# Sums of weights for the MLPs' up products, made by adding DMAs instead of VectorE

## The chip, the cores and the metric

The kernel runs on one core of a Trainium2 chip. The core has a matrix engine (TensorE, PE in the profile; PEld is its loading of weights), three engines for elementwise work (VectorE or DVE, ScalarE or ACT, GpSimd or POOL), and SyncE (SP), which here only issues DMAs. Each engine works through its own queue in order; 16 DMA engines move data between DRAM and the core's memory (SBUF). Matmul results land in PSUM, in banks of 128 x 512 numbers. The metric is device microseconds of one execution.

## What is computed

The reference is a trunk of two residual layers over 1024 tokens of width 1024 (latent attention in the first, an mLSTM in the second), each followed by a gated MLP with a causal convolution of width 3. The change is in the MLP's first half:

```
def conv_ffn(h, w_up, conv_w, conv_b, w_down):
    a, g = jnp.split(h @ w_up, 2, axis=-1)
    a = lax.conv_general_dilated(a, conv_w[:, None, :], window_strides=(1,),
                                 padding=[(CONV_W - 1, 0)],
                                 dimension_numbers=('NWC', 'WIO', 'NWC'),
                                 feature_group_count=D_FF) + conv_b
    return (jax.nn.gelu(a, approximate=False) * g) @ w_down
```

`w_up` is 1024 x 5632: 2816 columns for a and 2816 for the gate g.

## The kernel before

Products are taken in float32r in three parts (`mm3`, lines 171 to 182): each operand is split into a high part, which ACT makes by a copy that rounds, and a low part, which DVE makes by subtracting the high part from the source; the three matmuls are high x high, high x low and low x high.

**Tiling of the up products.** The 2816 columns of a and of g are cut into 22 groups of 128 each (`FT`), and the 1024 tokens into two halves of 512. Per group the product is a 2 x 2 block product: the blocks of weights are a's lower and upper 512 rows and g's lower and upper 512 rows; the blocks of h are the lower and upper rows of the first half of the tokens (B11, B21) and of the second (B12, B22). It is done in the Winograd form of Strassen's scheme, with seven block products instead of eight. Four of the weight operands are sums of blocks, and four of the operands of h (T1 to T4) are sums too; these last are made once per MLP (`operands_second`, lines 932 to 963), T2, T3 and T4 by a generator `rest`, of which a piece is run after products 7, 8 and 10 (`REST`, line 1272).

**One step** is a pair of functions (`steps`, line 1084): one makes the weight operand, one runs the block product of twelve matmuls and takes the result out of PSUM.

| step | weight operand made by | product | result |
|---|---|---|---|
| 1 | `w_a`: loads a's weights | p1, with B11 | ACT copies bank A to a1 |
| 2 | a's upper rows | p2, with B21 | DVE adds to a1 |
| 5 | `w_s1`: loads g's weights; sum S1 | p5, with T1 | ACT copies bank D to g2 |
| 3 | `w_s4`: two subtractions | p3, with B22, on top of D | ACT copies D to a2 |
| 6 | S2 (made in `w_s4`) | p6, with T2, on top of A | DVE adds A to a2; convolution, gelu |
| 7 | `w_s3`: one subtraction | p7, with T3, on top of A | DVE adds A to g2; times t2; store |
| 4 | g's upper rows | p4, with T4, on top of A | DVE multiplies with t1; store |

The four sums are the DVE instructions of lines 1000, 1006, 1007 and 1011. `wop` (line 983) makes the high and low part of a weight operand (lines 988 and 989) in one half of a pair of tiles; four pairs rotate, so eight operands are alive, and a new pair waits until both products of the old pair are done.

**The order** is a list `seq` written out by hand (lines 1090 to 1098). The first four groups (`AHEAD`) run products 1 and 2 first, which need only the first half of the tokens, and then go in pairs; after that group n runs 5, 1, (7 of n - 1), 2, (4 of n - 1), 3, 6. The loop at line 1259 makes weight operands some products ahead (`LOOK`: 7 ahead in the first eight, then 5) and runs the product. A planner then puts each engine's instructions in order by its own estimate of when they are ready; `tc.high_priority()` moves the takings out of PSUM forward. Hooks run at given places of the list: loads and operands for the down products near its end (`ends`).

**Loads and buffers.** Weights come by SP into tiles `raw` of 128 x 1024 (`RAWS` = 5 buffers), sums go to tiles `wsum` (tag `wraw`, 2 buffers; each held S1 or S2 in one half and the other sums in the other). Groups 0 to 3 load a's weights twice (`again`, line 1004). Results go to DRAM (`u_d`) and come back as q for the down products. POOL has nothing but a memset of two columns per group (line 1042) and a small power per norm (line 255) here; in the down products it makes low parts of weights.

Of the kernel before, what the change touches and what calls it, by code (L numbers as in the profile page):

```python
# [18 lines left out]
P = 128  # L19
# [78 lines left out]
def trunk_kernel(ctx: ExitStack, tc: tile.TileContext, xT, pos, c_d, cols_d, mod_w, win, winT, w0, w1, wf, wd, out):  # L98
# [4 lines left out]
    def nm(s):  # L103
        n_names[0] += 1
        return f"{s}_{n_names[0]}"
# [807 lines left out]
    def two(t, k):  # L913
        return t[:, k:k + 2, :]

    def split_two(t, k, src):
        act.activation(two(t[0], k), src, AF.Copy)
        dve.tensor_tensor(two(t[1], k), src, two(t[0], k).bitcast(F32), ALU.subtract)

    def split_t(t, j, src, eng):  # L920
        act.activation(t[0][:, j, :], src, AF.Copy)
        eng.tensor_tensor(t[1][:, j, :], src, t[0][:, j, :].bitcast(F32), ALU.subtract)

    def operands_first(x, rb, l, hh, hl):

        for k in range(0, KT, 2):
            by_rows(x, k, rb)
            for i in (k, k + 1):
                h_of(x, i, l, x[:, i, :])
            split_two((hh, hl), k, two(x, k))  # L930

    def operands_second(px, xs, rb, l, T):

        x1, x2 = xs
        for k in range(0, KT, 2):
            by_rows(x2, k, rb)
            for i in (k, k + 1):
                h_of(x2, i, l, x2[:, i, :])
        low = (0, 2)
        for k in low:  # L940
            dve.tensor_tensor(two(x1, k), two(x2, k), two(x1, k), ALU.subtract)
            split_two(T["T1"], k, two(x1, k))
        for k in low:
            split_two(T["B22"], k, two(x2, k + 4))

        def rest():
            yield
            for k in low:
                dve.tensor_tensor(two(x1, k), two(x2, k + 4), two(x1, k), ALU.subtract)
                split_two(T["T2"], k, two(x1, k))  # L950
            yield
            for k in low:
                dve.tensor_tensor(two(x2, k), two(x2, k + 4), two(x2, k), ALU.subtract)
                split_two(T["T3"], k, two(x2, k))
            yield
            t4 = block(0, [P, KT, HS], F32R, "T4")
            T["T4"] = t4[:, 0:4], t4[:, 4:8]
            for k in low:
                dve.tensor_tensor(two(x1, k), two(x1, k + 4), two(x1, k), ALU.subtract)
                split_two(T["T4"], k, two(x1, k))  # L960

        T["rest"] = rest()
        next(T["rest"])

    def mlp(px, psC, T, l, u_d, pd, done, cols, extra=None, scaled=None):
# [9 lines left out]
        def raw(m, i):  # L975
            t = px.tile([P, 1024], F32, tag="raw", bufs=RAWS, name=nm("raw"))
            nc.sync.dma_start(t, wf[l, m, i])
            return t
# [4 lines left out]
        def wop(src, eng):  # L983
            if not room:
                t = [wp.tile([P, 1024], F32R, tag=f"w{j}", bufs=wbufs, name=nm(f"w{j}")) for j in ("hi", "lo")]
                room.extend([x[:, i * HS:(i + 1) * HS] for x in t] for i in range(2))
            hi, lo = [v[:, 0:src.shape[-1]] for v in room.pop(0)]
            act.activation(hi, src, AF.Copy)  # L988
            eng.tensor_tensor(lo, src, hi.bitcast(F32), ALU.subtract)  # L989
            return hi, lo  # L990

        def w_a(g):
            g["ra"] = raw(g["m"], 0)
            return wop(g["ra"][:, 0:HS], dve)

        def w_s1(g):
            g["rg"] = raw(g["m"], 1)
            t = wp.tile([P, 1024], F32, tag="wraw", bufs=wraws, name=nm("wsum"))
            g["s"], g["t"] = t[:, 0:HS], t[:, HS:]
            dve.tensor_tensor(g["s"], g["rg"][:, 0:HS], g["rg"][:, HS:], ALU.add)  # L1000
            return wop(g["s"], dve)

        def w_s4(g):
            if g["again"]:
                g["ra"] = raw(g["m"], 0)
            dve.tensor_tensor(g["s"], g["s"], g["ra"][:, 0:HS], ALU.subtract)
            dve.tensor_tensor(g["t"], g["ra"][:, HS:], g["s"], ALU.subtract)
            return wop(g["t"], dve)

        def w_s3(g):  # L1010
            dve.tensor_tensor(g["t"], g["ra"][:, 0:HS], g["rg"][:, 0:HS], ALU.subtract)
            return wop(g["t"], dve)

        def prod(ps, w, t, first):
            need(T["B11" if t in ("B11", "B21") else "T1"])
# [36 lines left out]
        def p5(g, w):  # L1052
            g["D"] = bank("pd")
            prod(g["D"], w, "T1", True)
            g["g2"] = pf.tile([P, HS], F32, tag="g2", bufs=2, name=nm("g2"))
            with tc.high_priority():
                act.activation(g["g2"], g["D"], AF.Copy)

        def p3(g, w):
            prod(g["D"], w, "B22", False)  # L1060
            a = g["a2"] = half_a(g)
            dve.tensor_copy(a[:, 0:2], g["a1"][:, HS:HS + 2])
            with tc.high_priority():
                act.activation(a[:, 2:], g["D"], AF.Copy)

        def p6(g, w):
            prod(g["A"], w, "T2", False)
            with tc.high_priority():
                dve.tensor_tensor(g["a2"][:, 2:], g["a2"][:, 2:], g["A"], ALU.add)
            g["t1"] = conv(g, g.pop("a1"))  # L1070
            g["t2"] = conv(g, g.pop("a2"))

        def p7(g, w):
            prod(g["A"], w, "T3", False)
            with tc.high_priority():
                dve.tensor_tensor(g["g2"], g["g2"], g["A"], ALU.add)
            out(g, 1, g["t2"], g["g2"])

        def p4(g, w):
            prod(g["A"], w, "T4", False)  # L1080
            with tc.high_priority():
                out(g, 0, g["t1"], g["A"])

        steps = {1: (w_a, p1), 2: (lambda g: wop(g["ra"][:, HS:], dve), p2), 3: (w_s4, p3),
                 4: (lambda g: wop(g["rg"][:, HS:], dve), p4), 5: (w_s1, p5),
                 6: (lambda g: wop(g["s"], dve), p6), 7: (w_s3, p7)}


        groups = [{"m": m, "again": m < AHEAD} for m in range(FT)]
        seq = [(k, g) for g in groups[:AHEAD] for k in (1, 2)]  # L1090
        a, b = groups[0:2], groups[2:4]
        for k, pair in ((5, a), (3, a), (6, a), (7, a), ((5, 4), b), (3, b), (6, b), (7, b), (4, b)):
            seq += [(k, g) for g in pair] if k != (5, 4) else [(5, b[0]), (5, b[1]), (4, a[0]), (4, a[1])]
        for n in range(AHEAD, FT):
            prev = (lambda k: [(k, groups[n - 1])]) if n > AHEAD else lambda k: []
            g = groups[n]
            seq += [(5, g), (1, g), *prev(7), (2, g), *prev(4), (3, g), (6, g)]
        seq += [(k, groups[-1]) for k in (7, 4)]
        seq = [(lambda k=k, g=g: steps[k][0](g), lambda w, k=k, g=g: steps[k][1](g, w)) for k, g in seq]
        ends = {k: len(seq) - 1 - i for i, k in enumerate((4, 7, 6, 3, 0, 2, 0, 1, 5))}  # L1100
        hooks = {}

        def hook(i, fn):
# [678 lines left out]
```

## Time and profile before

| what | us |
|---|---|
| time, median of 3 runs (lowest to highest) | 2197.75 (2197.21 to 2198.31) |
| span of the profiled execution | 2200.1 |
| PE busy in the span | 2166.5 |
| DVE busy in the span | 1693.1 |
| ACT busy in the span | 1046.7 |
| POOL busy in the span | 178.3 |

The profiled execution is one of its own; beside its span no time of it is given. The page shows for each engine the time in which an instruction of it ran. Matmuls overlap (each takes some 0.39 us, but one starts every 0.23 us), so PE's busy time is the time in which at least one ran. Rows of groups give the line of the kernel, the engine, what it writes from what, how often, the busy time and the mean of one, and the idle time just before with what ended it. Rows of the timeline give the start, the duration, the engine and line, and in brackets the idle time before it. The first MLP's up products run from about 486 to 906 us of the span, the second's from about 1547 to 1967.

### The profile page before, as it was taken

The numbers are of one execution on the slowest core, as the hardware profiler recorded it, in microseconds if no ns is written. First come the engines' busy times: TensorE is split into PE (matmuls) and PEld (weight loads), VectorE is DVE, ScalarE is ACT, GpSimd is POOL, SyncE is SP. The second block draws the span as 40 slices with busy tenths as digits, with TensorE's granted clock in tenths as the row PEclk, the third lists the DMA queues.
The fourth block names the chain that finished last, engine by engine and source line by source line (L and its number), as shares of the span: only waits on it lengthen the run. The fifth ranks groups of instructions, "written<-read, shape, count | busy, mean of one in ns | idle before, by whom it ended". The sixth has DMA issues, their size and how long they took to land.

```text
span 2200.1 us, 28740 instructions
## 1 busy us (share of the span) xinstructions
PE 2166.5 (98%) x10557; PEld 1818.0 (83%) x10557; DVE 1693.1 (77%) x2769; ACT 1046.7 (48%) x1812; POOL 178.3 (8%) x216
## 2 busy tenths in 40 slices
PE   9999999999999999999999999999999999999998
PEld 7878888787888888877888888988788888887787
DVE  8877878669878777899973655566887777778997
ACT  6465556446544444543453434344554444453335
POOL 0000000000000000042210111010000000002232
PEclk9999999999999999999999999999999999999999
DMA  8512234832444332542132243444143332245122
GB/s 317 152 50 63 92 109 142 285 125 69 157 139 143 123 125 85 204 151 89 53 121 93 62 131 103 132 157 171 64 144 101 111 120 92 79 163 194 50 80 77
DMA packets 105085, 270.50 MB, mean 123 GB/s; under 512 B 12336, under 2 KB 15984, under 8 KB 104944
## 3 DMA queue, kind: packets, MB, share of 16 engines
q1 hardware_dynamic: 104544, 268.28, 36.9%
q8 instruction: 83, 1.36, 0.3%
q14 instruction: 58, 0.48, 0.1%
q10 hardware_dynamic: 400, 0.39, 0.1%
HBM read 221.53 MB, written 44.47 MB: 121 GB/s over the span
## 4 chain that ended last, share of the span: by engine, by line
PE 85%; DVE 9%; DMA 3%; ACT 2%; issue 1%; POOL 0%; SPq 0%; POOLq 0%; DVEq 0%; ACTq 0%
PE pa L175 7%; PE pa L177 7%; PE pa L176 7%; PE pd L177 3%; PE pd L175 3%; PE pd L176 3%; PE sc L673 3%; PE op L175 3%; PE op L176 3%; PE op L177 2%; PE inp L177 2%; PE da L175 2%; PE inp L175 2%; PE inp L176 2%; PE da L176 2%; PE db L175 2%
## 5 line engine op out<-in xcount | busy, mean ns | idle before, releaser
L988 ACT ACTIVATE whi<-raw 128x512 fp32r<-128x512 f32 (+1 forms) x252 | 147.3, 607 | 243.2 <-PE pb L176 61.0
L988 ACT ACTIVATE whi<-wsum 128x512 fp32r<-128x512 f32 (+1 forms) x224 | 134.0, 617 | 181.8 <-PE pa L176 61.5
L175 PE MATMUL pa<-T,whi 128*128 128x512 f32 x528 | 205.9, 390 | 0.0
L176 PE MATMUL pa<-T,whi 128*128 128x512 f32 x528 | 205.4, 389 | 0.0
L177 PE MATMUL pa<-T,wlo 128*128 128x512 f32 x528 | 205.1, 389 | 0.0
L989 DVE TENSOR_TENSOR wlo<-wsum,whi 128x512 fp32r<-128x512 f32 (+1 forms) x224 | 151.1, 690 | 32.8 <-ACT whi L988 31.5
L989 POOL TENSOR_TENSOR wlo<-raw,whi 128x512 fp32r<-128x512 f32 (+1 forms) x80 | 119.9, 1515 | 401.7 <-ACT whi L988 394.0
L175 PE MATMUL da<-U,whi 128*128 128x512 f32 (+1 forms) x364 | 139.5, 383 | 3.4 <-DVE x L294 3.4
L177 PE MATMUL da<-U,wlo 128*128 128x512 f32 (+1 forms) x364 | 138.4, 383 | 2.0 <-DVE wlo L989 2.0
L176 PE MATMUL da<-U,whi 128*128 128x512 f32 (+1 forms) x364 | 139.2, 382 | 0.0
L989 DVE TENSOR_TENSOR wlo<-raw,whi 128x512 fp32r<-128x512 f32 (+1 forms) x172 | 115.7, 679 | 24.9 <-ACT whi L988 24.9
L167 ACT ACTIVATE whi<-wraw 128x1024 fp32r<-128x1024 f32 x67 | 70.7, 1059 | 117.1 <-PE op L176 59.2
L175 PEld LDWEIGHTS pa<-T,whi 128*128 128x128 f32 x528 | 99.1, 188 | 22.2 <-ACT whi L988 1.2
L177 PEld LDWEIGHTS pa<-T,wlo 128*128 128x128 f32 x528 | 99.1, 188 | 20.6
L176 PEld LDWEIGHTS pa<-T,whi 128*128 128x128 f32 x528 | 99.1, 188 | 20.3
L1140 DVE TENSOR_TENSOR U<-q,U 128x1024 fp32r<-128x1024 f32 x84 | 102.9, 1241 | 14.0 <-ACT U L1139 13.6
L1028 ACT ACTIVATE ct<-a,cols 128x512 f32<-128x512 f32 x88 | 70.8, 808 | 83.9 <-DVE a L1050 47.9
L175 PE MATMUL db<-U,whi 128*128 128x512 f32 x264 | 103.3, 391 | 1.3 <-ACT whi L988 1.3
L168 DVE TENSOR_TENSOR wlo<-wraw,whi 128x1024 fp32r<-128x1024 f32 x67 | 81.7, 1222 | 29.4 <-ACT whi L167 27.2
L177 PE MATMUL db<-U,wlo 128*128 128x512 f32 x264 | 102.9, 390 | 0.0
L176 PE MATMUL db<-U,whi 128*128 128x512 f32 x264 | 102.8, 389 | 0.0
L1139 ACT ACTIVATE U<-q 128x1024 fp32r<-128x1024 f32 x84 | 79.7, 979 | 47.7 <-DVE q L1138 22.2
(378 smaller groups left out, 6097.3 us busy)
## 6 DMA issues: line engine op xcount, KB each, us to landing
raw<-in_wf SPq DMA_DIRECT2D x96, 512.0 KB, 4.0
wraw<-in_w SPq DMA_DIRECT2D x67, 512.0 KB, 3.7
mraw<-in_mod_w SPq DMA_DIRECT2D x56, 512.0 KB, 4.0
ud<-ct SPq DMA_DIRECT2D x88, 256.0 KB, 2.4
q<-ud SPq DMA_DIRECT2D x88, 256.0 KB, 4.6
raw<-in_wd SPq DMA_DIRECT2D x32, 512.0 KB, 6.4
pa<-in_mod_w SPq DMA_DIRECT2D x24, 512.0 KB, 3.7
x<-xd SPq DMA_DIRECT2D x48, 256.0 KB, 4.8
```

Of the source, the lines that this page charges most:

```text
L167: act.activation(hi, raw, AF.Copy)
L168: dve.tensor_tensor(lo, raw, hi.bitcast(F32), ALU.subtract)
L175: pe.matmul(ps, lh, rh, start=first, stop=False, skip_group_check=more)
L176: pe.matmul(ps[:, 0:rl.shape[-1]], lh, rl, start=False, stop=False, skip_group_check=more)
L177: pe.matmul(ps, ll, rh, start=False, stop=last, skip_group_check=more)
L673: pe.matmul(ps[:, cs], a[:, qs if n < 3 else qrs_], b[:, cs], start=n == 0, stop=n == 4)
L988: act.activation(hi, src, AF.Copy)
L989: eng.tensor_tensor(lo, src, hi.bitcast(F32), ALU.subtract)
L1028: act.activation(t, a[:, 2:], AF.Identity, bias=col(f"cb{l}", m), scale=cw(m, 2))
L1139: act.activation(hi, w, AF.Copy)
L1140: dve.tensor_tensor(lo, w, hi.bitcast(F32), ALU.subtract)
```

## The change

The sums of weights are all made with plus signs, so that a DMA that adds to its destination can make them: `add_dma` issues from POOL a DMA with `accum_op=ALU.add`, which reads a block of weights in DRAM and adds it to what lies in SBUF. S1 is loaded as g's lower rows by SP, then g's upper rows are added. Step 5 splits it; then a's lower rows are added, which gives the operand of step 6; step 6 splits it; then a's upper rows are added, which gives the operand of step 3. The operand of step 7 is g's lower rows with a's lower rows added to them in place. To keep the result the same, the signs of T1, T2 and T4 are turned, g2 is taken with a factor of -1, the sum of product 7 is subtracted, and the last multiplication has a factor of -1 (`scalar_tensor_tensor` for `tensor_tensor`).

With it change: the order of steps 3 and 6 (6 first), and so T2 is made at once and B22 by the first piece of `rest`; a2 is copied from bank A after product 6, and D is added to it by DVE after product 3; two groups share a tile `wsum`, one half each; the loads of a group (a's and g's weights, the sum's first block and the two first adds) are issued ahead, at step 5 of the group before, or for the first groups at places given in `ahead` (`load`, `load_s`); the second load of a's weights for groups 0 to 3 is gone. Per group there are one more plain load of 256 KB on SP and four adding DMAs of 256 KB on POOL, and the four sums on DVE are gone.

```diff
...
         act.activation(t[0][:, j, :], src, AF.Copy)
         eng.tensor_tensor(t[1][:, j, :], src, t[0][:, j, :].bitcast(F32), ALU.subtract)
+    def neg_sub(out, a, b):
+        dve.scalar_tensor_tensor(out, a, -1.0, b, ALU.mult, ALU.subtract)
+    def add_dma(t, src):
+        pool.dma_start(t, src, accum_op=ALU.add)
     def operands_first(x, rb, l, hh, hl):
         for k in range(0, KT, 2):
...
                 h_of(x2, i, l, x2[:, i, :])
         low = (0, 2)
         for k in low:
-            dve.tensor_tensor(two(x1, k), two(x2, k), two(x1, k), ALU.subtract)
+            dve.tensor_tensor(two(x1, k), two(x1, k), two(x2, k), ALU.subtract)
             split_two(T["T1"], k, two(x1, k))
         for k in low:
-            split_two(T["B22"], k, two(x2, k + 4))
+            neg_sub(two(x1, k), two(x1, k), two(x2, k + 4))
+            split_two(T["T2"], k, two(x1, k))
         def rest():
             yield
             for k in low:
-                dve.tensor_tensor(two(x1, k), two(x2, k + 4), two(x1, k), ALU.subtract)
-                split_two(T["T2"], k, two(x1, k))
+                split_two(T["B22"], k, two(x2, k + 4))
             yield
             for k in low:
                 dve.tensor_tensor(two(x2, k), two(x2, k + 4), two(x2, k), ALU.subtract)
...
             t4 = block(0, [P, KT, HS], F32R, "T4")
             T["T4"] = t4[:, 0:4], t4[:, 4:8]
             for k in low:
-                dve.tensor_tensor(two(x1, k), two(x1, k + 4), two(x1, k), ALU.subtract)
+                neg_sub(two(x1, k), two(x1, k), two(x1, k + 4))
                 split_two(T["T4"], k, two(x1, k))
         T["rest"] = rest()
...
             eng.tensor_tensor(lo, src, hi.bitcast(F32), ALU.subtract)
             return hi, lo
+        halves_ = []
+        def load_a(g):
+            g["ra"] = raw(g["m"], 0)
+        def load_s(g):
+            m = g["m"]
+            if not halves_:
+                t = wp.tile([P, 1024], F32, tag="wraw", bufs=wraws, name=nm("wsum"))
+                halves_.extend(t[:, i * HS:(i + 1) * HS] for i in range(2))
+            g["rg"], g["s"] = raw(m, 1), halves_.pop(0)
+            nc.sync.dma_start(g["s"], wf[l, m, 1][:, 0:HS])
+            add_dma(g["s"], wf[l, m, 1][:, HS:])
+            add_dma(g["rg"][:, 0:HS], wf[l, m, 0][:, 0:HS])
+        def load(g):
+            load_a(g)
+            load_s(g)
         def w_a(g):
-            g["ra"] = raw(g["m"], 0)
+            if "ra" not in g:
+                load_a(g)
             return wop(g["ra"][:, 0:HS], dve)
         def w_s1(g):
-            g["rg"] = raw(g["m"], 1)
-            t = wp.tile([P, 1024], F32, tag="wraw", bufs=wraws, name=nm("wsum"))
-            g["s"], g["t"] = t[:, 0:HS], t[:, HS:]
-            dve.tensor_tensor(g["s"], g["rg"][:, 0:HS], g["rg"][:, HS:], ALU.add)
-            return wop(g["s"], dve)
-        def w_s4(g):
-            if g["again"]:
-                g["ra"] = raw(g["m"], 0)
-            dve.tensor_tensor(g["s"], g["s"], g["ra"][:, 0:HS], ALU.subtract)
-            dve.tensor_tensor(g["t"], g["ra"][:, HS:], g["s"], ALU.subtract)
-            return wop(g["t"], dve)
-        def w_s3(g):
-            dve.tensor_tensor(g["t"], g["ra"][:, 0:HS], g["rg"][:, 0:HS], ALU.subtract)
-            return wop(g["t"], dve)
+            w = wop(g["s"], dve)
+            add_dma(g["s"], wf[l, g["m"], 0][:, 0:HS])
+            return w
+        def w_s2(g):
+            w = wop(g["s"], dve)
+            add_dma(g["s"], wf[l, g["m"], 0][:, HS:])
+            return w
         def prod(ps, w, t, first):
             need(T["B11" if t in ("B11", "B21") else "T1"])
...
             prod(g["D"], w, "T1", True)
             g["g2"] = pf.tile([P, HS], F32, tag="g2", bufs=2, name=nm("g2"))
             with tc.high_priority():
-                act.activation(g["g2"], g["D"], AF.Copy)
-        def p3(g, w):
-            prod(g["D"], w, "B22", False)
+                act.activation(g["g2"], g["D"], AF.Copy, scale=-1.0)
+        def p6(g, w):
+            prod(g["A"], w, "T2", False)
             a = g["a2"] = half_a(g)
             dve.tensor_copy(a[:, 0:2], g["a1"][:, HS:HS + 2])
             with tc.high_priority():
-                act.activation(a[:, 2:], g["D"], AF.Copy)
-        def p6(g, w):
-            prod(g["A"], w, "T2", False)
+                act.activation(a[:, 2:], g["A"], AF.Copy)
+        def p3(g, w):
+            prod(g["D"], w, "B22", False)
             with tc.high_priority():
-                dve.tensor_tensor(g["a2"][:, 2:], g["a2"][:, 2:], g["A"], ALU.add)
+                dve.tensor_tensor(g["a2"][:, 2:], g["a2"][:, 2:], g["D"], ALU.add)
             g["t1"] = conv(g, g.pop("a1"))
             g["t2"] = conv(g, g.pop("a2"))
         def p7(g, w):
             prod(g["A"], w, "T3", False)
             with tc.high_priority():
-                dve.tensor_tensor(g["g2"], g["g2"], g["A"], ALU.add)
+                dve.tensor_tensor(g["g2"], g["g2"], g["A"], ALU.subtract)
             out(g, 1, g["t2"], g["g2"])
         def p4(g, w):
             prod(g["A"], w, "T4", False)
             with tc.high_priority():
-                out(g, 0, g["t1"], g["A"])
-        steps = {1: (w_a, p1), 2: (lambda g: wop(g["ra"][:, HS:], dve), p2), 3: (w_s4, p3),
+                t = g["t1"]
+                dve.scalar_tensor_tensor(t, g["A"], -1.0, t, ALU.mult, ALU.mult)
+                nc.sync.dma_start(u_d[g["m"]][0], t)
+        steps = {1: (w_a, p1), 2: (lambda g: wop(g["ra"][:, HS:], dve), p2), 3: (lambda g: wop(g["s"], dve), p3),
                  4: (lambda g: wop(g["rg"][:, HS:], dve), p4), 5: (w_s1, p5),
-                 6: (lambda g: wop(g["s"], dve), p6), 7: (w_s3, p7)}
-        groups = [{"m": m, "again": m < AHEAD} for m in range(FT)]
+                 6: (w_s2, p6), 7: (lambda g: wop(g["rg"][:, 0:HS], dve), p7)}
+        groups = [{"m": m} for m in range(FT)]
         seq = [(k, g) for g in groups[:AHEAD] for k in (1, 2)]
         a, b = groups[0:2], groups[2:4]
-        for k, pair in ((5, a), (3, a), (6, a), (7, a), ((5, 4), b), (3, b), (6, b), (7, b), (4, b)):
+        for k, pair in ((5, a), (6, a), (3, a), (7, a), ((5, 4), b), (6, b), (3, b), (7, b), (4, b)):
             seq += [(k, g) for g in pair] if k != (5, 4) else [(5, b[0]), (5, b[1]), (4, a[0]), (4, a[1])]
         for n in range(AHEAD, FT):
             prev = (lambda k: [(k, groups[n - 1])]) if n > AHEAD else lambda k: []
             g = groups[n]
-            seq += [(5, g), (1, g), *prev(7), (2, g), *prev(4), (3, g), (6, g)]
+            seq += [(5, g), (1, g), *prev(7), (2, g), *prev(4), (6, g), (3, g)]
         seq += [(k, groups[-1]) for k in (7, 4)]
-        seq = [(lambda k=k, g=g: steps[k][0](g), lambda w, k=k, g=g: steps[k][1](g, w)) for k, g in seq]
-        ends = {k: len(seq) - 1 - i for i, k in enumerate((4, 7, 6, 3, 0, 2, 0, 1, 5))}
+        ahead = {(1, 2): lambda: load_s(groups[0]), (1, 3): lambda: load_s(groups[1]),
+                 (6, 0): lambda: load_s(groups[2]), (6, 1): lambda: load_s(groups[3])}
+        for n in range(AHEAD, FT):
+            ahead[(6, 2) if n == AHEAD else (5, n - 1)] = lambda n=n: load(groups[n])
+        def make_w(k, g):
+            w = steps[k][0](g)
+            if (k, g["m"]) in ahead:
+                ahead[k, g["m"]]()
+            return w
+        seq = [(lambda k=k, g=g: make_w(k, g), lambda w, k=k, g=g: steps[k][1](g, w)) for k, g in seq]
+        ends = {k: len(seq) - 1 - i for i, k in enumerate((4, 7, 3, 6, 0, 2, 0, 1, 5))}
         hooks = {}
         def hook(i, fn):
```

## What is predicted, and from what

> **What bounds the kernel now.** I read the page first: engine totals, then the chain that ended last.
>
> ```profile
> span 2200.1 us, 28740 instructions
> ...
> PE 2166.5 (98%) x10557; PEld 1818.0 (83%) x10557; DVE 1693.1 (77%) x2769; ACT 1046.7 (48%) x1812; POOL 178.3 (8%) x216
> ...
> PE 85%; DVE 9%; DMA 3%; ACT 2%; issue 1%; POOL 0%; SPq 0%; POOLq 0%; DVEq 0%; ACTq 0%
> ```
>
> PE is idle for 2200.1 - 2166.5 = 33.6 us of the whole span, and the change takes no matmul away: seven products of twelve matmuls per group stay. So the most that any relief of DVE can bring is PE's idle time in the MLPs. The DVE share of the chain, 9%, is not a saving: it passes through DVE also where PE had other work. Next, busy time by stretches: the crowded start of the first MLP's up products, one group of the steady part, and the steady part as a whole.
>
> ```profile
> core 0: us, PE busy (x) PEld busy (x) DVE busy (x) ACT busy (x) POOL busy (x), PEclk, DMA share, GB/s
> 500.00:540.00 40.00, 38.90 (x170) 31.30 (x169) 39.71 (x52) 25.67 (x36) 0.00 (x0) 1.00 0.14 42
> 750.00:769.00 19.00, 19.00 (x86) 15.73 (x85) 14.18 (x24) 8.60 (x15) 0.10 (x1) 1.00 0.42 135
> 560.00:884.00 324.00, 324.00 (x1431) 268.30 (x1430) 253.23 (x414) 143.39 (x240) 1.59 (x16) 1.00 0.39 127
> ```
>
> In the steady part PE is busy 324.00 of 324.00 us while DVE has 71 us to spare (253.23 busy). 1431 matmuls in 324 us are 0.2264 us each, so a product is 2.72 us and a group of 84 matmuls 19.0 us. DVE bounds nothing there. Only the start is short of DVE (39.71 of 40 us), and PE idles 1.10 us in it. The waits of PE, by whom it waited for, say how much there is to win:
>
> ```profile
> PE da L175 <- DVE x L294: 3.4, 5, 1.0
> ...
> PE da L177 <- DVE wlo L989: 2.0, 2, 1.0
> ...
> PE pd L175 <- ACT whi L988: 1.9, 2, 0.9
> ...
> PE db L175 <- ACT whi L988: 1.3, 2, 0.6
> ...
> PE pd L177 <- DVE wlo L989: 0.3, 2, 0.2
> ```
>
> The two rows of pd are the starts of the two MLPs: 2.2 us together. The rows of da and db, 6.7 us, lie in the down products, after the last sum of weights of the up part.
>
> **The change, part by part.** First the four sums that leave DVE, and the forms that grow.
>
> ```profile
> L1007 DVE TENSOR_TENSOR wsum<-raw,wsum 128x512 f32<-128x512 f32 x44 | 30.3, 688 | 0.6
> ...
> L1006 DVE TENSOR_TENSOR wsum<-wsum,raw 128x512 f32<-128x512 f32 x44 | 30.2, 687 | 0.3
> L1011 DVE TENSOR_TENSOR wsum<-raw,raw 128x512 f32<-128x512 f32 x44 | 30.2, 690 | 1.1
> ...
> L1000 DVE TENSOR_TENSOR wsum<-raw 128x512 f32<-128x512 f32 x44 | 30.1, 687 | 0.5
> ...
> L1035 DVE TENSOR_TENSOR ct<-ct,pa 128x512 f32<-128x512 f32 x44 | 30.0, 681 | 0.1
> ...
> L1030 DVE SCALAR_TENSOR_TENSOR ct<-a,cols,ct 128x512 f32<-128x512 f32 x88 | 65.6, 749 | 1.5
> ```
>
> Removed: 30.3 + 30.2 + 30.2 + 30.1 = 120.8 us of DVE. Added: the last product's multiply becomes a scalar-tensor-tensor, 44 x (749 - 681) ns = 3.0 us. The subtractions of h change form or operands only, and the factor -1 on ACT's copies adds no instruction. Net 118 us less DVE, all beside a PE that is full: worth 0 in the steady part. If that cover were absent it would be 2.7 us per group.
>
> At the start it is worth something. These are rows of the timeline of DVE, ACT and PE:
>
> ```profile
> 528.30 1.29 DVE L1000 TENSOR_TENSOR wsum<-raw 128x512 f32<-128x512 f32 x2
> ...
> 528.42 1.06 ACT L917 ACTIVATE T<-o 128x1024 fp32r<-128x1024 f32 x1 [1.02 <-DVE o L959]
> 529.38 1.13 ACT L988 ACTIVATE whi<-wsum 128x512 fp32r<-128x512 f32 x2
> ...
> 530.05 0.50 PE L175 MATMUL pd<-T,whi 128*128 128x512 f32 x1 [0.94 <-ACT whi L988]
> ...
> 531.99 0.50 PE L177 MATMUL pd<-T,wlo 128*128 128x512 f32 x1 [0.16 <-DVE wlo L989]
> ```
>
> PE waits for product 5 of the third group, whose sum DVE makes late, at 528.30. That sum goes to a DMA, and so do six others that DVE makes between 500 and 528, by the groups of that stretch:
>
> ```profile
> L1006 DVE TENSOR_TENSOR wsum<-wsum,raw 128x512 f32<-128x512 f32 x2 | 1.4, 685 | 0.0
> ...
> L1007 DVE TENSOR_TENSOR wsum<-raw,wsum 128x512 f32<-128x512 f32 x2 | 1.4, 684 | 0.0
> ...
> L1011 DVE TENSOR_TENSOR wsum<-raw,raw 128x512 f32<-128x512 f32 x2 | 1.4, 682 | 0.0
> ```
>
> 3 x 1.4 = 4.2 us and half of the pair at 528.30, 0.6 us, stand no longer ahead of the split. DVE, and ACT which waits for it, then come up to 4.8 us earlier, and the wait of 0.94 + 0.16 = 1.10 us goes with over 3 us to spare. The move of T2 ahead of B22 brings two subtractions of 1.22 us forward but sends two splits back; the operands stay ahead. I count **-1.1 us per MLP, -2.2 us** in all.
>
> The DMAs. Every group gets one plain 256 KB load on SP and four accumulating ones on POOL; eight reloads of 512 KB go.
>
> ```profile
> raw<-in_wf SPq DMA_DIRECT2D x96, 512.0 KB, 4.0
> ...
> q<-ud SPq DMA_DIRECT2D x88, 256.0 KB, 4.6
> ```
>
> In the group quoted above, 0.42 x 19.0 = 8.0 us of DMA time moved 135 GB/s x 19 us = 2.57 MB, 3.1 us per MB. Five times 0.262 MB at that price is 4.1 us: the share goes from 0.42 to (8.0 + 4.1)/19 = 0.64. The engines fill where an add costs over (19.0 - 8.0 - 0.8)/3.26 = 3.1 times a copy, 3.26 us being four adds at the copy's price. No row prices an add: it is bounded by one copy below and, above, by nothing that the trace shows; I take one to two copies, a share of 0.64 to 0.81, since it moves the same bytes and reads as many more. [...]
>
> The latency of one add, L, from POOL's release to landing: no row shows an accumulating DMA. Below, a 256 KB transfer in 2.0 us; above, two of the slowest 256 KB loads in a row, 2 x 7.3 = 14.6 us. These rows are the issue-to-landing times of ud and of q, and with them one load of the first groups and POOL's small operation, which are used below:
>
> ```profile
> DMA to landing us min/median/max: 2.0/2.4/5.7
> ...
> DMA to landing us min/median/max: 2.5/4.6/7.3
> ...
> 473.70 0.33 SPq L977 DMA_DIRECT2D raw<-in_wf  x1
> ...
> 490.00 1.01 POOL L255 TENSOR_TENSOR rstd<-var,nhalf 128x4 f32<-128x4 f32 x1 [38.57 <-DVE var L254]
> ```
>
> I take the nearest row, a load of 256 KB from DRAM, 4.6 us, plus a second read of 0.262 MB (0.8 us) plus 1.0 us for POOL's own work, as its small operation above: **L = 6.4 us**.
>
> What waits for it. Three of four adds have five products (13.6 us) or more before their sum is split. The tight one is in step 6: DVE's low part of the sum must be done, then POOL adds, and step 3, the very next, splits the result. Step 3's ACT copy then stands in ACT's queue with the copies of pd and pa behind it, and its DVE subtraction ahead of the update of g (L1076), for which PE waits before product 4. In every second group the two steps get their weight buffers together; the rows (today 3 and 6, then 6 and 3):
>
> ```profile
> 767.62 0.63 ACT L988 ACTIVATE whi<-wsum 128x512 fp32r<-128x512 f32 x1 [1.19 <-PE pd L176]
> ...
> 768.29 0.69 DVE L989 TENSOR_TENSOR wlo<-wsum,whi 128x512 fp32r<-128x512 f32 x1 [0.78 <-ACT whi L988]
> ...
> 778.67 0.69 DVE L1076 TENSOR_TENSOR g<-g,pa 128x512 f32<-128x512 f32 x1 [2.19 <-PE pa L177]
> ...
> 781.19 0.39 PE L175 MATMUL pa<-T,whi 128*128 128x512 f32 x1
> ```
>
> The add can start at 768.98. PE needs the update by 781.19, so L1076 may start at 780.5, the subtraction before it at 779.9, the copy before that at 779.2. **Slack: 779.2 - 768.98 = 10.2 us**, against L = 6.4. ACT would stand still for 6 us of 19, of which it is busy 8.6; it has the room. In the other groups step 3's buffer comes a product pair later and the slack is larger. So this costs nothing up to L = 10.2 us.
>
> POOL's queue is now in order behind adds that wait for loads; behind them stand only memsets of 0.1 us and, at the start, L255 at 490.00. The sixth load of weights, the first that has to wait for a buffer, is issued at 473.70 and lands in 4.0 us, so the adds of the first two groups are out before it. SP gets three more issues less one reload; an issue behind a store that waits for DVE is late by at most that wait, and the loads have a whole group (19 us) of lead. I value both at 0; uncovered they are the third rival.
>
> The sum: -2.2 + 0 + 0 = -2.2 us. The span, 2200.1, is 2.35 us above the median of the runs; no other time of the profiled execution is given, so I take the difference over: 2197.75 - 2.2 = **2195.6 us**.
>
> **The rivals.** The bound for a difference that a measurement of this kernel can tell is 0.2%, 4.4 us.
>
> One, *the add between steps 6 and 3 becomes the wait*. Decides from L = 10.2 us. For it: the DMA engines go from 0.42 to 0.64 or more, and POOL's adds stand in order behind others. Against: even the slowest 256 KB load of this trace took 7.3 us. At L = 12.2 PE loses 2 us in every second of the 18 steady groups, in two MLPs: 2 x 9 x 2 = 36, so 2231.6 us. It reaches 4.4 x 18 = 79 us at L = 14.6. Chance 0.18.
>
> Two, *the DMA engines become the bound*. Decides where an add costs over 3.1 copies. At five: 8.0 + 0.8 + 16.3 = 25.1 us per group, 6.1 over, 44 times: +268 us, about 2464. Nothing in the profile prices an add, so it stays open. Chance 0.08.
>
> Three, *the first groups start late*: an add on POOL holds L255. T1 is ready at 505.39 and wanted at 509.91, as these rows show, so 4.5 us are spare; a hold of 8 us (L and a landing's rest) costs 3.5 us per MLP and hides the gain: 2197.75 + 7 = 2204.8. Chance 0.07.
>
> ```profile
> 504.17 1.22 DVE L918 TENSOR_TENSOR T<-o,T 128x1024 fp32r<-128x1024 f32 x1
> ...
> 509.91 0.39 PE L175 MATMUL pd<-T,whi 128*128 128x512 f32 x1
> ```
>
> Four, *the relief reaches the down products* and their 6.7 us of waits go too: 2195.6 - 6.7 = 2188.9. Against: at 903.86 DVE itself waits 1.65 us for PE, so no backlog is carried over. Chance 0.07.
>
> ```profile
> 903.86 0.69 DVE L1069 TENSOR_TENSOR a<-a,pa 128x512 f32<-128x512 f32 x1 [1.65 <-PE pa L177]
> ```
>
> Five, *the relief at the start doesn't come*, because the added load is as late as the sum was: 2197.8. Chance 0.05.
>
> [...]
>
> **The numbers.** Forecast 0.55, rivals 0.18, 0.08, 0.07, 0.07, 0.05. Within 0.2%: 0.55 + 0.05 = 0.60; faster 0.07; slower 0.18 + 0.08 + 0.07 = 0.33. The forecast's own range is 2193.4 to 2199. The range for 8 in 10 goes from 2189 (rival four) to 2232 (rival one at L = 12.2, about half of its chance): 0.55 + 0.05 + 0.07 + 0.07 + 0.09 = 0.83.
>
> **What would show it.** Right: in the steady part PE busy throughout, DVE down by 2.7 us per group, ACT waiting for a DMA of wsum for a few us in every second group with no PE wait behind it, DMA share 0.6 to 0.8, and no wait of pd at the start. Wrong: PE waits on pa, pd or pb behind L988 or the update of g in the steady part (rival one); DMA share near 1 (two); L255 late at the start (three). A landing time of the adds above 10 us would break the forecast.

## The result and the profile after

The changed kernel takes 2250.6 us (median of four runs, 2246.85 to 2254.86) against 2197.5 us before (2194.85 to 2198.31): a ratio of 1.0246, 95% interval 1.0232 to 1.0261, **slower by 53 us**. The forecast was 2195.6 us, its range ended at 2232.

The page after, against the lines shown of before:

```profile
span 2248.0 us, 29031 instructions
...
PE 2181.1 (97%) x10557; PEld 1824.6 (81%) x10557; DVE 1584.7 (70%) x2593; ACT 1040.4 (46%) x1812; POOL 332.5 (15%) x392
...
q0 software_dynamic: 25344, 46.15, 13.0%
...
wsum<-in_wf POOLq DMA_DIRECT2D x132, 256.0 KB, 5.5
```

DVE is 108 us lighter, where 118 were forecast, and the span is 47.9 us longer. (The profiled execution of before, 2200.1 us, is longer than any of its timed runs, so 48 of the 53 us can be followed here.) Where PE lost it is in the waits (us in total, times, longest) and, second fence, in the windows (busy time of PE, PEld, DVE, ACT and POOL, then granted clock, DMA share and GB/s):

```profile
POOL raw L930 <- DMA raw<-in_wf: 252.1, 30, 41.3
...
ACT whi L996 <- DMA wsum<-in_wf: 188.3, 53, 9.2
...
POOL wsum L930 <- DMA wsum<-in_wf: 86.5, 14, 14.1
...
PE pa L175 <- DVE g L1096: 28.6, 14, 5.2
...
PE pa L175 <- ACT a L1084: 5.0, 2, 2.7
```

```profile
560.00:884.00 324.00, 303.39 (x1295) 247.28 (x1294) 191.57 (x314) 127.36 (x218) 55.47 (x76) 0.97 0.70 181
...
1620.00:2000.00 380.00, 369.35 (x1601) 303.12 (x1600) 222.53 (x357) 164.29 (x278) 66.12 (x91) 0.99 0.64 159
...
560.00:564.00 4.00, 0.32 (x2) 0.00 (x0) 0.00 (x0) 1.22 (x2) 0.00 (x0) 1.00 0.49 79
564.00:568.00 4.00, 2.45 (x6) 1.96 (x7) 3.85 (x7) 2.31 (x5) 0.00 (x0) 0.51 0.09 36
568.00:572.00 4.00, 4.00 (x13) 3.14 (x12) 2.46 (x4) 0.00 (x0) 2.03 (x3) 0.64 0.82 210
572.00:576.00 4.00, 4.00 (x19) 3.32 (x18) 0.42 (x1) 1.08 (x3) 0.68 (x2) 1.00 1.09 258
```

PE now waits 28.6 + 5.0 = 33.6 us on bank A in the up products, where it did not wait before; the pd waits of 2.2 us are gone. The rest is slower matmuls: at 0.2264 us each, the 1295 and 1601 matmuls of the two long windows would take 293.2 and 362.5 us, and PE was busy for 303.4 and 369.4, so 17 us more. The short windows show why: after a wait of 5.2 us that ended at 565.55, the granted clock is 0.51 and 0.64 in the two windows of four us that follow. 33.6 - 2.2 + 17.1 = 48.5, about the span's 47.9.

The chain behind that longest wait, in the timeline of the changed kernel:

```profile
550.72 0.93 SPq L985 DMA_DIRECT2D raw<-in_wf  x2
...
553.17 0.69 DVE L997 TENSOR_TENSOR wlo<-wsum,whi 128x512 fp32r<-128x512 f32 x1 [1.22 <-ACT whi L996]
...
556.78 0.86 POOL L930 DMA_DIRECT2D raw<-in_wf  x1 [3.18 <-DMA raw<-in_wf]
...
558.90 0.89 POOL L930 DMA_DIRECT2D wsum<-in_wf  x1 [1.26 <-DVE a L1089]
...
562.78 0.63 ACT L996 ACTIVATE whi<-wsum 128x512 fp32r<-128x512 f32 x1 [5.24 <-DMA wsum<-in_wf]
563.32 0.80 ACT L1048 ACTIVATE ct<-a,cols 128x512 f32<-128x512 f32 x1
...
564.15 0.75 DVE L1049 SCALAR_TENSOR_TENSOR ct<-a,cols,ct 128x512 f32<-128x512 f32 x1 [4.36 <-ACT ct L1048]
564.82 0.68 DVE L1096 TENSOR_TENSOR g<-g,pa 128x512 f32<-128x512 f32 x1
...
565.55 0.80 PE L175 MATMUL pa<-T,whi 128*128 128x512 f32 x1 [5.23 <-DVE g L1096]
```

The sum is that of group 4, the first steady one, between steps 5 and 6. DVE is done with the old sum at 553.86 and the next add could go. But POOL stands at the add for step 7 of a later group (raw), whose load SP issued only at 550.72; then 1.26 us more; the add goes out at 558.90 and lands just before 562.78. ACT stands still for 5.24 us at the split that needs it; the convolution's first copy (L1048) is queued behind the split, DVE's L1049 waits for that copy, and the update of g (L1096), which has nothing to do with the sum, is queued behind L1049. PE waits for the update. This shows how a late sum reaches PE; the hold on POOL is not the only thing that makes it late, as e1 shows.

The adds themselves, by the rows of line 930:

```profile
L930 POOL DMA_DIRECT2D wsum<-in_wf x132: 856/883/1440, 463.5 to 1991.0; - x132
...
DMA to landing us min/median/max: 3.5/5.2/9.6
```

The 5.2 us count from the start of the issue, so POOL's 0.9 us lie in them: the add issued at 558.90 has landed by 562.78. The page's 5.5 us are the median of the 132 adds into `wsum` alone. The prediction took L = 6.4.

### The profile page after: what moved, and what is told of

Its sections match the earlier page's. It is cut to its first block, busy times and chain, and to the rows that moved or that the text cites. A ratio compares the mean times of both kernels' runs of the same rounds, so it can differ in the third digit from the quotient of the medians.

```text
span 2248.0 us, 29031 instructions
## 1 busy us (share of the span) xinstructions
PE 2181.1 (97%) x10557; PEld 1824.6 (81%) x10557; DVE 1584.7 (70%) x2593; ACT 1040.4 (46%) x1812; POOL 332.5 (15%) x392
## 2 busy tenths in 40 slices
DMA packets 135614, 324.00 MB, mean 144 GB/s; under 512 B 15728, under 2 KB 19376, under 8 KB 135472
## 5 line engine op out<-in xcount | busy, mean ns | idle before, releaser
L996 ACT ACTIVATE whi<-raw 128x512 fp32r<-128x512 f32 (+1 forms) x296 | 172.0, 608 | 194.8 <-DVE raw L1206 48.6
L175 PE MATMUL pa<-T,whi 128*128 128x512 f32 x528 | 212.2, 402 | 33.6 <-DVE g L1096 28.6
L996 ACT ACTIVATE whi<-wsum 128x512 fp32r<-128x512 f32 (+1 forms) x180 | 107.1, 616 | 292.7 <-DMA wsum<-in_wf 188.3
L997 DVE TENSOR_TENSOR wlo<-wsum,whi 128x512 fp32r<-128x512 f32 (+1 forms) x180 | 120.3, 679 | 154.7 <-ACT whi L996 154.6
L176 PE MATMUL pa<-T,whi 128*128 128x512 f32 x528 | 210.5, 399 | 0.0
L177 PE MATMUL pa<-T,wlo 128*128 128x512 f32 x528 | 210.2, 398 | 0.0
L930 POOL DMA_DIRECT2D wsum<-in_wf x132 | 122.2, 990 | 452.8 <-DVE wlo L997 293.9
L997 DVE TENSOR_TENSOR wlo<-raw,whi 128x512 fp32r<-128x512 f32 (+1 forms) x216 | 145.4, 679 | 28.0 <-ACT whi L996 27.9
L175 PEld LDWEIGHTS pa<-T,whi 128*128 128x128 f32 x528 | 101.9, 193 | 62.3 <-DVE g L1096 35.2
L1048 ACT ACTIVATE ct<-a,cols 128x512 f32<-128x512 f32 x88 | 70.9, 811 | 112.1 <-DVE a L1070 61.6
L176 PEld LDWEIGHTS pa<-T,whi 128*128 128x128 f32 x528 | 101.9, 193 | 21.0
```

The source lines that it names most:

```text
L175: pe.matmul(ps, lh, rh, start=first, stop=False, skip_group_check=more)
L176: pe.matmul(ps[:, 0:rl.shape[-1]], lh, rl, start=False, stop=False, skip_group_check=more)
L177: pe.matmul(ps, ll, rh, start=False, stop=last, skip_group_check=more)
L930: pool.dma_start(t, src, accum_op=ALU.add)
L1048: act.activation(t, a[:, 2:], AF.Identity, bias=col(f"cb{l}", m), scale=cw(m, 2))
```

## The experiments

Times are medians; each ratio is to the kernel before, timed beside it on the same chip. Those medians of before were 2195.5 to 2196.5 us.

**e1.** The add for step 7 is forced behind the tight add (the one between steps 6 and 3) in POOL's queue; the planner, which goes by its own estimate of when an instruction is ready, had put it in front.

```diff
+            with tc.issue_after(behind["add2"].ins) if behind else ExitStack():
+                add_dma(g["rg"][:, 0:HS], wf[l, g["m"], 0][:, 0:HS])
...
+            if n > AHEAD:
+                ahead[6, n - 1] = lambda n=n: load_r(groups[n], groups[n - 1])
```

> Theories, for all four runs. Queue: the add between steps 6 and 3 is late because POOL issues its DMAs in order, and the add for step 7 of the next group, which waits for a load (30 holds, 252.1 us in the changed kernel), stands ahead of it; the add itself takes what was estimated, about 0.9 us of issue and 5.5 us to landing. Latency: the add between steps 6 and 3 is too slow wherever it stands in the queue. Traffic: the added DMA work slows loads and stores that others wait for. Order: taking step 6 before step 3 and T2 before B22 is what costs. This run moves the add for step 7 behind the add of step 6 in POOL's queue, a group later, and changes nothing else. Queue: POOL's holds on raw go, and PE's waits of 28.6 us behind the update of g with them: 2196 to 2212 us. Latency, Traffic and Order: no change, 2243 to 2255 us.

Measured 2223.7 us, ratio 1.0127 (1.0109 to 1.0145). Half of the loss goes with one place in a queue, which none of Latency, Traffic and Order gives; but half stays, so Queue in this form is not all. The waits of this run:

```profile
POOL wsum L930 <- DMA wsum<-in_wf: 62.2, 12, 13.3
...
POOL raw L930 <- DMA raw<-in_wf: 51.5, 4, 41.4
...
PE pa L175 <- DVE g L1101: 13.2, 7, 4.4
```

POOL's holds on raw fell from 30 to 4; holds by the first add of a later group, which waits for the plain load on SP, remain. And a wait can stay without a hold. This is the add of the chain above in e1:

```profile
555.20 0.69 DVE L997 TENSOR_TENSOR wlo<-wsum,whi 128x512 fp32r<-128x512 f32 x1 [1.22 <-ACT whi L996]
...
556.30 0.86 POOL L930 DMA_DIRECT2D wsum<-in_wf  x1 [0.67 <-DVE wlo L997]
...
564.71 0.63 ACT L996 ACTIVATE whi<-wsum 128x512 fp32r<-128x512 f32 x1 [5.14 <-DMA wsum<-in_wf]
...
567.48 0.79 PE L175 MATMUL pa<-T,whi 128*128 128x512 f32 x1 [4.44 <-DVE g L1101]
```

POOL issues it 0.4 us after the sum is free, but it takes 8.4 us to land, and PE waits 4.44 us where it waited 5.23.

**e2.** The tight sum is made by DVE.

```diff
-            add_dma(g["s"], wf[l, g["m"], 0][:, HS:])
...
+            dve.tensor_tensor(g["s"], g["s"], g["ra"][:, HS:], ALU.add)
```

> The sum for step 3 is made by DVE (44 tensor-tensor adds of 0.69 us), the other three stay adding DMAs; queue order of the rest as in the changed kernel. Queue and Latency: nothing tight is left on POOL, 2195 to 2203 us. Traffic: one add of four less, so about a quarter of the loss comes back, 2233 to 2245 us. Order: no change, 2243 to 2255 us.

Measured 2213.1 us, 1.0073 (1.0056 to 1.009): between all the expectations. What is left are two PE waits in each MLP, at its start (532.31, 1.81 us; 563.74, 3.92 us; 1602.60 and 1633.34 in the second).

**e3.** New signs and order, all sums on DVE: `dve.tensor_tensor(g["s"], g["s"], g["ra"][:, 0:HS], ALU.add)` and three like it in place of the adds.

> New signs, new forms of T2 and T4 and the new order of steps, with all four sums made by DVE from loaded weights and no adding DMA; loads as in the kernel before. Order: 2235 to 2255 us. Queue, Latency, Traffic: as before, 2195 to 2200 us (DVE has 0.07 us more work in each of 44 last products).

Measured 2200.0 us, 1.0019 (1.0009 to 1.0028). Order falls.

**e4.** e3 with one plain load and four adding DMAs per group into tiles that nobody reads.

> The kernel of the run before plus one plain load of 256 KB and four adding DMAs of 256 KB per group whose results nobody reads: the DMA work of the change without anyone waiting for it. Traffic: slower by tens of us, 2225 to 2255. Queue and Latency: 2195 to 2203 us, with a DMA share of 0.55 to 0.75 in the steady part. Order: the same as the run before, whatever that gives.

Measured 2212.9 us, 1.0073 (1.0057 to 1.009): 13 us for DMA work alone, less than Traffic and more than Queue said. PE's waits in it stand between 560 and 635 us and at 1628 and 1660, the start again. There the loads of weights (line 985) are slow: between 520 and 640 us they land in 7.2 us at the median and 11.8 at most, against 3.9 and 5.4 in e3, and ACT waits 5.40 us for one at 553.58.

**e5 and e6.** The sums of the first five groups are made by DVE, in the changed kernel (e5) and in e2's (e6):

```diff
-            w = steps[k][0](g)
+            w = first_sum(g, k) if g["m"] <= AHEAD and k in (5, 6, 3, 7) else steps[k][0](g)
```

> What stands after four runs: of the change's loss, 27 us go when the add for step 7 no longer stands ahead of the tight add, 11 us more go when the tight sum is made by DVE, and 17 us are left, with PE's last waits all at the start of the steady part (at 532 and 564 us and the same in the second MLP). Theory Start: those 17 us are the adds of the first five groups, where steps 7 and 4 of a group before are missing between the steps and the slack is small. Rival Traffic: they are the added DMA work, wherever it stands. This run is the changed kernel with the sums of the first five groups made by DVE. Start: about 17 us less than the changed kernel, 2230 to 2239 us. Traffic: 4 of 44 adds' share, under 5 us less, 2245 to 2252 us.

> The kernel with the tight sum on DVE, and besides all sums of the first five groups on DVE; the other 17 groups of an MLP keep one plain load and three adding DMAs. Start: 2195 to 2203 us, no PE wait behind the update of g left. Traffic: 2207 to 2214 us.

e5: 2230.6 us, 1.0157 (1.0135 to 1.0179); e6: 2201.6 us, 1.0027 (1.0017 to 1.0037). Both as Start says. The windows of e6 also show what the relief of DVE is worth: in the steady part DVE is busy 222 us where it was 253 before, and PE is as full as it was.

```profile
560.00:884.00 324.00, 324.00 (x1431) 268.28 (x1430) 222.16 (x361) 142.92 (x238) 43.53 (x64) 1.00 0.66 178
```

**e7.** Both edits, e1's and e5's; the tight add stays a DMA in 17 groups per MLP.

> The kernel with the add for step 7 behind the tight add, and besides all sums of the first five groups on DVE; the tight add stays a DMA in the other groups. If the three parts add up: 2196 plus 11 for the tight add itself, 2203 to 2212 us, with PE's waits behind the update of g of 2 to 6 us left in the steady part. If the queue's hold was all there is to the steady part: 2195 to 2202 us. Traffic: 2216 to 2224 us.

Measured 2206.9 us, 1.0055 (1.0038 to 1.0073), as the sum of the parts.

**e8.** e1 with step 6 two products earlier:

```diff
-            seq += [(5, g), (1, g), *prev(7), (2, g), *prev(4), (6, g), (3, g)]
+            seq += [(5, g), (1, g), *prev(7), (6, g), (2, g), *prev(4), (3, g)]
```

> The kernel with the add for step 7 behind the tight add, and besides step 6 taken two products earlier in each steady group, so that step 3 comes three products (8.2 us) behind it instead of one; sums all by adding DMAs. If the 11 us are the tight add's own time, the added 5.4 us of room take most of it away and the start's 17 us stay: 2210 to 2218 us. If the room between the steps doesn't matter (the adds are late for another reason, such as the loads): 2219 to 2228 us.

Measured 2223.4 us, 1.0125 (1.011 to 1.0141): no gain over e1, in the range for "the room doesn't matter". It is not clean, since the room that step 3 gets is taken from step 6, which now comes three products after step 5 instead of five. In its trace ACT's longest wait for a sum in the first MLP, 8.79 us to 682.58, follows adds that POOL issued at 672.38 after 11.99 us of standing still.

**e9 and e11.** e7 with the sum for step 5 made by DVE, so that neither the plain load of s on SP nor the add that waits for it is left. In e9 the add for step 7 still goes out a group early: its sum for step 5 contains a's lower rows in addition, and DVE waits for that add. In e11 it goes out behind the tight add of its own group.

```diff
-            nc.sync.dma_start(g["s"], wf[l, m, 1][:, 0:HS])
-            add_dma(g["s"], wf[l, m, 1][:, HS:])
...
+            dve.tensor_tensor(g["s"], g["rg"][:, 0:HS], g["rg"][:, HS:], ALU.add)
```

And e11 against e9:

```diff
-                ahead[6, n - 1] = lambda n=n: load_r(groups[n], groups[n - 1])
+            ahead[6, n] = lambda n=n: load_r(groups[n], groups[n])
```

> The kernel with the add for step 7 behind the tight add and the first five groups on DVE (2206.9 us), and besides the sum for step 5 made by DVE in the other groups: the plain load of 256 KB on SP and the add that waits for it on POOL are gone, the adds for steps 6, 3 and 7 stay. That add is issued for two groups at once and in every second group stands ahead of the tight add (POOL waits 5 times, 34.4 us, for such loads in the first MLP). If the rest of the steady part's loss is this second hold in POOL's queue: 2196 to 2203 us, no PE wait behind the update of g. If it is the tight add's own issue and landing of 6 to 7 us: 2204 to 2210 us, as without the edit.

> The run with the sum for step 5 on DVE, with the add for step 7 now issued behind the tight add of its own group, so that the sum for step 5 reads the loaded halves and waits for no add. On POOL stay the adds for steps 6, 3 and 7 of the groups from the sixth on; no plain load on SP, nothing on POOL that waits for a load. If the rest of the steady part's loss was a hold in POOL's queue by adds that wait for loads: 2196 to 2202 us. If it is the tight add's own issue and landing: 2203 to 2212 us, with ACT waiting for wsum some 15 times or more per MLP as without the edit (17 times, 51.6 us).

e9: 2212.4 us, 1.0068 (1.0056 to 1.0081), outside both expectations, since its sum has a wait that was not meant. e11: 2202.4 us, 1.0031 (1.0019 to 1.0043), between the two stated ranges, so the time alone doesn't decide; its waits in the steady part (560 to 884 us) do:

```profile
ACT whi L996 <- DMA wsum<-in_wf: 42.3, 16, 6.2
...
PE pa L175 <- DVE g L1114: 0.6, 2, 0.4
```

ACT still waits for the adds 16 times, 2.6 us on average, which was to be the sign of the tight add's own time. But PE waits 0.6 us in all, against 2.2 in e7: with nothing in its way the tight add is hidden from PE. The adds also land sooner with fewer DMAs beside them (a DMA share of 0.64 in the steady part, 0.70 in the changed kernel): the median of those into `wsum` is 4.0 us here, 4.9 in e7 and 5.5 in the changed kernel.

**e10.** e5 with both parts of step 3's split on POOL, so that neither ACT nor DVE has an instruction waiting for the tight add.

```diff
+            pool.tensor_tensor(hi, g["s"], nought[0], ALU.add)
+            pool.tensor_tensor(lo, g["s"], hi.bitcast(F32), ALU.subtract)
```

> The changed kernel with the first five groups on DVE (2230.6 us), the adds as late as there, but the split of step 3's weights (high and low part) made by POOL in the other groups, so that neither ACT nor DVE has an instruction that waits for the tight add. Theory In order: PE is late because ACT and DVE stand still behind that wait and the convolution and the update of g queue up behind it, while the weights themselves are made five products ahead; PE's waits behind the update of g go and the time is 2197 to 2212 us. Rival Late weights: PE lacks the weights of step 3 themselves; PE waits for them instead, 2226 us or more (POOL's two operations are slower, 1.7 us each by its low parts in the down products).

Measured 2217.0 us, 1.0084 (1.0067 to 1.0101): 13.6 us less than e5, between the two ranges. In the second MLP PE's waits behind the update of g fall from 5 (5.0 us) to one, quoted from e10's timeline; in the first, 5 are left, and there DVE also stands still for rows of the modulation whose loads are late, from e10's waits between 470 and 960 us (0.8 us in the kernel before).

```profile
1638.74 0.50 PE L175 MATMUL pa<-T,whi 128*128 128x512 f32 x1 [0.31 <-DVE g L1124]
```

```profile
DVE mraw L198 <- DMA mraw<-in_mod_w: 29.6, 11, 5.9
...
PE pa L175 <- DVE g L1124: 10.4, 5, 4.0
```

So In order is borne out in the second MLP. In the first it is not decided: 10.4 us of these waits are left of e5's 12.4, and that the late rows are their cause is argued, not shown. PE waits for the update of g, not for weights, in both MLPs; Late weights falls.

**e12.** e4's unread DMAs from the sixth group on only.

> The kernel with the new signs and order and all sums on DVE (2200.0 us), plus one plain load and four adding DMAs per group that nobody reads, from the sixth group on only. In the run with these in all groups (2212.9 us) PE's waits in the first MLP stand between 560 and 635 us. Theory Start for the DMA work: in the steady part it costs nothing, 2198 to 2204 us. Theory Traffic: 17 of 22 groups of those 13 us, 2208 to 2213 us.

Measured 2202.0 us, 1.0031 (1.0019 to 1.0042), as Start says, with the engines' DMA share at 0.75 in the steady part:

```profile
560.00:884.00 324.00, 322.95 (x1422) 266.51 (x1421) 250.03 (x411) 141.62 (x237) 60.43 (x83) 1.00 0.75 194
```

| kernel | us | what goes |
|---|---|---|
| changed | 2250.6 | |
| e5: first five groups on DVE | 2230.6 | -20.0 |
| e7: and the add for step 7 behind the tight add | 2206.9 | -23.7 |
| e11: and the sum for step 5 on DVE | 2202.4 | -4.5 |
| e3: no adding DMA | 2200.0 | -2.4 |
| before | 2196.5 | -3.5 |

The step from e11 to e3 is smaller than these runs can separate; the last one is small, but e3's interval is clear of 1. The parts overlap: e1's edit alone brings 26.9 us and e2's 37.5. No version tried is faster than the kernel before.

## Why the prediction was wrong

**What held.** PE bounds the kernel (busy 97% of the span), and the relief of DVE in the steady part is worth nothing (e6: DVE busy 222 us for 253, PE 324.00 of 324.00 in both). L = 6.4 us: measured 5.2 at the median, 5.5 for the adds into `wsum`, but up to 9.6. The DMA share of 0.64 to 0.81: 0.70 here, 0.75 in e12. In the steady part DMA work that nobody waits for costs nothing that these runs can separate (e12 is 2.0 us above e3). Where the adds land soon, the tight one fits its room: in e11 it is there in 17 groups of 22 and costs PE 0.6 us in the steady part of the first MLP.

**What failed first**: "Slack: 779.2 - 768.98 = 10.2 us". The prediction read the path behind the tight add too short. It let PE go on 2.0 us after ACT begins to split the tight sum (779.2 to 781.19), with nothing but this split's subtraction ahead of the update of g. These are rows of a steady group of the changed kernel:

```profile
769.89 0.68 DVE L997 TENSOR_TENSOR wlo<-wsum,whi 128x512 fp32r<-128x512 f32 x1
...
770.98 0.86 POOL L930 DMA_DIRECT2D wsum<-in_wf  x1 [5.86 <-DVE wlo L997]
...
778.45 1.15 ACT L996 ACTIVATE whi<-wsum 128x512 fp32r<-128x512 f32 x2 [7.71 <-DMA wsum<-in_wf]
...
780.35 0.75 DVE L1049 SCALAR_TENSOR_TENSOR ct<-a,cols,ct 128x512 f32<-128x512 f32 x1
...
783.11 0.69 DVE L997 TENSOR_TENSOR wlo<-raw,whi 128x512 fp32r<-128x512 f32 x1 [1.22 <-ACT whi L996]
...
784.11 0.69 DVE L997 TENSOR_TENSOR wlo<-raw,whi 128x512 fp32r<-128x512 f32 x1 [0.31 <-ACT whi L996]
784.72 0.68 DVE L1096 TENSOR_TENSOR g<-g,pa 128x512 f32<-128x512 f32 x1
...
785.45 0.50 PE L175 MATMUL pa<-T,whi 128*128 128x512 f32 x1 [2.93 <-DVE g L1096]
```

From the split to PE it is 7.0 us: a convolution and two more splits, all of which need ACT first, stand ahead of the update. In other groups it is 5.0 (842.16 to 847.18). The sum was free at 770.57 and split at 778.45, 7.9 us later, and PE waited 2.9: the room is 5.0 us here, and 5 to 7 us at the other tight adds that PE waited for. An add of 5.5 us just fits or just doesn't, and whatever makes it later is paid by PE. Two things did.

One is "I value both at 0", said of POOL's queue and SP's. The prediction said that POOL is now in order behind adds that wait for loads, and then looked behind them only for memsets and L255. Behind them also stand the other adds, the tight one among them. SP's lead of "a whole group" was not there either: in the chain at 565.55, the load was issued 6 us before the add that needs it. By the trace, five of PE's waits, 15.3 us, stand behind an add that went out 3.8 to 5.0 us after its sum was free, each right behind an add for step 7. ACT and DVE, too, let nothing past the instruction that waited in that chain: 3.18 us of standing still on POOL, 5.24 on ACT and 4.36 on DVE, one behind the other.

The other is the spread of the landing times, of which L took one value. Eight waits, 13.1 us, stand behind an add that POOL issued 0.4 us after its sum was free, as the one at 770.98, and that took 6.3 to 8.2 us to land. The edits of e7 and e11 take the holds away and bring 28 us of the 53. Since the adds also land sooner in these runs, the two parts are not separated.

**What failed second**: "Three of four adds have five products (13.6 us) or more before their sum is split" and "the slack is larger", said of the other groups. In group 4, the first steady one, the products 7 and 4 of a group before are missing, so step 6 comes three products after step 5; and the first groups run in pairs with reloads and q around them. PE's waits of 2.3 us at 530.77 and 5.2 us at 565.55 stand there, and 20 us go in e5. It is not slack alone: the DMA engines are crowded there too (a share of 0.91 between 540 and 560 us, 0.50 in e3). Unread DMAs in these groups cost 11 us (e4 against e12), and without a hold the add of e1 took 8.4 us to land. How much of the 20 us is which stays open. The gain at the start, -2.2 us, did come as a wait (no pd row after) and was overrun.

**Rival one** had the right place, PE at the update of g before product 4, with the wrong deciding point: no add took 10.2 us to land and it happened all the same, since the room is 5 to 7 us. That its price of 2 us per second group, 36 in all, is near the 33.6 us of waits is luck: 13.6 of these stand at the start of the two MLPs, where it had none. The 17 us of slower matmuls were in no term of it.

**What stands between the sum and PE** is the order of ACT's and DVE's queues and not a lack of weights: the weights were being made products ahead of their use, and in e10, where POOL splits the tight sum, PE's waits for the update in the second MLP fall from 5.0 to 0.3 us and none for weights comes in their place.

**Left open**: the 3.5 us of e3 over before (its profiled span, 2198.4, is not longer than before's 2200.1, so the trace shows no place for them); what brings the 4.5 us of e11, the sum for step 5 on DVE or the new place of the add for step 7; what holds PE in e10's first MLP; and the wait of 1.26 us at 558.90, put down to an instruction of DVE that has no visible part in it.

## What to carry to other kernels

When work moves to a queue that nearly idles, list what will stand in front of each of its instructions and when that can go; an early prefetch ahead of a tight transfer makes the tight one wait for the prefetch's own load (e1's edit, which ends that, brings 26.9 us). Ask the same of the engine that takes the result: its wait stops everything queued behind, which here was the update that PE needed (ACT stood still for 5.24 us and PE for 5.23 in the chain at 565.55). So count the room up to the instruction that the bottleneck waits for, with all that stands in the queues between, and set the spread of the landing times against it, not one value. An engine off the critical path was no gain to relieve (31 us less of DVE in e6, PE as full), and the groups at the edge of a loop, where neighbours are missing, had the least room (20.0 us go in e5).

## What was not expected of the hardware

Some waits of PE here cost more than themselves. The 5.2 us wait was followed by half the clock: the 0.51 and 0.64 of its two windows put the return to full speed at about 570.9. The trace has six more stretches at half the clock in the up products, of 3.4 us each and each after a wait of 1.97 to 3.36 us; with the first it is 27 us in all. PE was idle for 1.5 us of them, so by estimate, (27 - 1.5)/2, they cost about 13 of the 17 us; 2.6 more come from the last matmul before each of the 16 waits, which counts for 0.39 us instead of 0.23. Before the last stretch stands a wait of 1.97 us, which ended at 1826.10:

```profile
1823.60:1827.00 3.40, 1.43 (x7) 0.88 (x6) 2.91 (x5) 2.15 (x5) 0.00 (x0) 1.00 0.30 49
1827.00:1830.40 3.40, 3.40 (x10) 2.62 (x9) 3.40 (x7) 0.81 (x1) 0.00 (x0) 0.50 0.61 204
```

Waits of 2.3 us at 530.77 and 2.2 us at 763.19 brought none. So the length of one wait does not decide it; what does, these runs do not show.

An adding DMA costs the DMA engines about two copies, by an estimate from the shares. Between e3 and e12 the share in the steady part rises from 0.39 to 0.75: 0.36 x 19 = 6.8 us per group for a load and four adds; less 0.8 for the load (0.262 MB at the 3.1 us per MB of before), 1.5 us per add, 1.9 times a copy of 0.8.

In e10 a subtraction of DVE took 1.60 us beside a tensor operation of POOL, as two rows of its timeline show; the one before it, at 685.86, took 0.69, and the mean of this form is 799 ns in e10 and 684 in the changed kernel:

```profile
686.34 1.56 POOL L1059 TENSOR_TENSOR wlo<-wsum,whi 128x512 fp32r<-128x512 f32 x1
...
686.86 1.60 DVE L997 TENSOR_TENSOR wlo<-raw,whi 128x512 fp32r<-128x512 f32 x1 [0.31 <-ACT whi L996]
```

That POOL's operation is the cause is not shown.
